# Masks added to bias tables by transfers, keys split once for two heads and stacked by transfers, in a two-layer decoder kernel

## The chip, the cores and the metric

The kernel runs on one core of a Trainium2 chip. PE (TensorE) multiplies, DVE (VectorE), ACT (ScalarE) and POOL (GpSimd) work element by element, and SP and POOL issue transfers (DMA) between DRAM and the on-chip memory. The metric is the time of one execution on the device in microseconds (us). The median of three runs before the change is 1831.09 us (1829.66 to 1831.96).

## The reference, cut to what matters

The input is one sequence of 512 positions with 1024 features, all in float32. Layer 0 has a feed-forward, the first ("hybrid") mixer and a second feed-forward; layer 1 has a feed-forward, the sliding mixer and a last feed-forward.

```python
h = h + 0.5 * swiglu(rmsnorm(h, g[0]), w1[0], w3[0], w2[0])
h = h + mixer(rmsnorm(h, g[1]))          # hybrid in layer 0, sliding in layer 1
h = h + 0.5 * swiglu(rmsnorm(h, g[2]), w1[1], w3[1], w2[1])
...
# the hybrid mixer: heads 0 to 7 (A) and 8 to 15 (B)
cq = rmsnorm(cq, cq_g); qb = cq @ wq_b; q_idx = cq @ wq_idx
o_a = dilated_mixture(qa, ka, va, table[:, :8])
sc = relu(einsum('bqhd,bsd->bqhs', q_idx, k_idx))         # 8 index heads
score = einsum('bqhs,bqh->bqs', sc, w_idx) * idx_scale    # one score per query and key
_, idx = top_k(score, 128)                                # 128 keys for each query
logits = q @ k[idx] * 64 ** -0.5 + bias                   # heads B see only these keys
o_b = softmax(logits) @ v[idx]
return concat(o_a, o_b) @ w_out
```

Every head has 64 features and a bias that depends on the distance of query and key. The B heads see only the selected keys, which the kernel does with masks of 512 x 512 instead of a gather.

## The kernel before

**Precision.** Operands of a product are split into a high and a low part (in `d4` and `s2` buffers of 32-bit numbers), and three products (low x high, high x low, high x high) replace one. In the listings these are L389, L390 and L391 for projections, L613 to L615 for the feed-forwards and L869 to L871 for the output projection. A weight of a mixer is loaded by SP (L338), cast to its high part on ACT (L356), copied with a factor of -1 (L357), and POOL then issues a transfer that adds the weight a second time to that negative (L359): what remains is the low part. A function `unit` with `lands=True` does this.

**Order.** Everything is emitted as operations of a planner (`Plan`). It takes them by due time `v`, keeps for each engine a modelled clock, and gives out buffers from pools: 58 slots of `s2` (128 x 512), 20 of `d4` (128 x 1024), 8 banks, and 2 value buffers `v` in a pool of their own. `LIMIT` says how many of a kind may be held, `RESERVE` how many slots a kind must leave free. The order that comes out is fixed, and each engine runs its instructions in that order. So an instruction that waits holds up all behind it on its engine, and so does a transfer on SP's or POOL's queue. A load is given the slot of a buffer that another instruction still reads and waits for that.

**Entry of a mixer.** The last feed-forward products of w2 give the eight chunks of x one after another. For each, DVE adds (L685), ACT scales it (L410) and squares it (L426), DVE makes the low part (L411) and adds up the squares (L427). L452 is a product with ones that sums the squares over the features. It needs the last chunk's L427. From it DVE computes the root (L435 to L441), PE and ACT spread it (L457, L462), and the projections are multiplied by it.

**First mixer.** `hybrid` (L879) does the index scores (L964 on PE, L967 on ACT, L971 to L978 on DVE), and then eight rounds of two heads: `project(j)` makes values, keys and queries, `attend(j)` two heads, `out_proj` a share of the output. In the queue of DVE between these stands the selection: for each of three blocks of 128 queries (256, 384 and 512 keys; the first block needs none) 16 times MAX8 (L986) and MATCH_REPLACE8 (L988). `close` makes a bf16 mask (L994) from what was replaced. Tables of the bias are loaded by `toeplitz` (L691, one transfer of 256 KB a head).

In `head`, each block of queries has two products of keys and queries (L780, L781), then L787 on DVE adds the bias table and takes the minimum. For the eight B heads (j of 4 and more) a third product, of the identity `identb` with the mask (L783), adds the mask to the scores on PE, for 256, 384 and 512 keys. ACT takes the exponential, DVE the reciprocal (L806), ACT or POOL scale (L817, L813), PE transposes (L829), L845 and L846 multiply with the values.

**Keys.** `k_stack` (L713) makes of one projection two stacks, one for each head, each with the keys (high and low) in both halves of the partitions, because queries hold their high part in one half and their low part in the other. Per pair: one product (L717), two casts of 64 x 512 (L399, ACT), two copies into the other half (L725 on ACT or L728 on POOL), four subtractions of 64 x 512 (L325, DVE or POOL). It is called eight times here and once in `sliding` (L1044).

## Time and profile before

| | |
|---|---|
| median of the runs | 1831.09 us (1829.66 to 1831.96) |
| the profiled execution | 1832.38 us, its span 1830.6 us |
| granted TensorE clock, mean | 0.995 |
| busy: PE, DVE, ACT, POOL | 1807.2, 1319.3, 969.2, 170.5 us |
| share of the chain that ended last: PE, DVE, ACT, DMA | 89%, 4%, 3%, 2% |

The profile is of one execution. "Idle before" is the time an engine stood still before an instruction, with what ended it. Busy times of PE are of pipelined products whose ends are modelled: one product of 512 columns is shown as 0.39 us long, and in a dense stretch they follow each other every 0.23 us.

### The profile page before, as it was taken

What the parts mean: (1) busy time and instruction counts of PE and PEld (TensorE: products, weight loads), DVE (VectorE), ACT (ScalarE), POOL (GpSimd) and SP (SyncE); (2) the same over time, 40 slices, a digit from 0 to 9 for tenths busy, and PEclk for the clock granted to TensorE, in tenths of its full rate; (3) what the DMA queues carried; (4) which work ended last, traced back from release to release, by engine and by line L of the source; (5) the groups of instructions that cost most, each with busy time, mean ns of one, the idle gap of its engine ahead of it and who ended that gap; (6) DMA issues with size and microseconds to landing.
All of it is one profiled execution on the core that took longest, in us unless ns stands there. A gap on an engine that the chain in (4) does not pass through costs nothing.

```text
span 1830.6 us, 28269 instructions
## 1 busy us (share of the span) xinstructions
PE 1807.2 (99%) x11036; PEld 1612.7 (88%) x11036; DVE 1319.3 (72%) x2225; ACT 969.2 (53%) x1600; POOL 170.5 (9%) x228
## 2 busy tenths in 40 slices
PE   9999999999999999999999999999999999999997
PEld 6889989888878889998998989989788889899896
DVE  8575857559977897586588866848468798577483
ACT  6343625658768555253355534625679755255263
POOL 2100000115524000000000000000124200000000
PEclk9999999999999999999999999999999999999999
DMA  6713423785745314232343224313844523243231
GB/s 215 245 58 114 122 64 113 198 209 119 162 112 138 103 48 126 92 105 81 109 117 97 83 91 127 118 56 105 229 95 102 150 70 116 70 127 116 70 104 46
DMA packets 75141, 211.55 MB, mean 116 GB/s; under 512 B 12976, under 2 KB 17168, under 8 KB 75008
## 3 DMA queue, kind: packets, MB, share of 16 engines
q1 hardware_dynamic: 58176, 176.88, 30.6%
q0 software_dynamic: 16688, 32.85, 9.8%
q8 instruction: 86, 1.41, 0.3%
q14 instruction: 47, 0.39, 0.1%
q10 hardware_dynamic: 144, 0.03, 0.0%
HBM read 205.92 MB, written 8.47 MB: 117 GB/s over the span
## 4 chain that ended last, share of the span: by engine, by line
PE 89%; DVE 4%; ACT 3%; DMA 2%; issue 1%; POOL 0%; SPq 0%; DVEq 0%; ACTq 0%; POOLq 0%
PE ps L389 14%; PE ps L390 14%; PE ps L391 14%; PE ps L613 12%; PE ps L615 12%; PE ps L614 12%; DVE d L325 1%; PE ps L869 1%; PE ps L870 1%; PE ps L871 1%; PE ps L829 1%; ACT s L796 1%; DMA d<-in_w 1%; PE ps L1155 1%; PE ps L1157 1%
## 5 line engine op out<-in xcount | busy, mean ns | idle before, releaser
L325 DVE TENSOR_TENSOR d<-d,d 128x1024 fp32r<-128x1024 f32 (+3 forms) x415 | 448.8, 1096 | 186.6 <-ACT d L346 138.3
L346 ACT CAST d<-d 128x1024 fp32r<-128x1024 f32 (+3 forms) x415 | 388.0, 949 | 328.6 <-DMA d<-in_w 209.0
L613 PE MATMUL ps<-s,d 128*128 128x256 f32 x1904 | 539.5, 283 | 0.0
L615 PE MATMUL ps<-s,d 128*128 128x256 f32 x1904 | 538.8, 283 | 0.0
L614 PE MATMUL ps<-s,d 128*128 128x256 f32 x1904 | 538.8, 283 | 0.0
L389 PE MATMUL ps<-s,d 128*128 128x512 f32 (+1 forms) x1252 | 496.0, 396 | 2.2 <-DVE d L325 2.0
L390 PE MATMUL ps<-s,d 128*128 128x512 f32 (+1 forms) x1252 | 489.8, 391 | 0.4 <-DVE s L411 0.3
L391 PE MATMUL ps<-s,d 128*128 128x512 f32 (+1 forms) x1252 | 489.2, 391 | 0.0
L613 PEld LDWEIGHTS ps<-s,d 128*128 128x128 f32 x1904 | 365.4, 192 | 0.5
L614 PEld LDWEIGHTS ps<-s,d 128*128 128x128 f32 x1904 | 365.4, 192 | 0.4
L615 PEld LDWEIGHTS ps<-s,d 128*128 128x128 f32 x1904 | 365.4, 192 | 0.0
L391 PEld LDWEIGHTS ps<-s,d 128*128 128x128 f32 (+1 forms) x1252 | 235.8, 188 | 50.2
L389 PEld LDWEIGHTS ps<-s,d 128*128 128x128 f32 (+1 forms) x1252 | 236.2, 189 | 49.7 <-DVE d L325 2.9
L390 PEld LDWEIGHTS ps<-s,d 128*128 128x128 f32 (+1 forms) x1252 | 236.2, 189 | 46.9 <-DVE s L411 1.2
L626 ACT COPY d<-ps 128x512 f32<-128x512 f32 x136 | 79.8, 587 | 250.0 <-PE ps L615 249.7
L685 DVE SCALAR_TENSOR_TENSOR s<-ps,s 128x512 f32<-128x512 f32 x88 | 60.7, 690 | 140.9 <-PE ps L391 140.9
L325 DVE TENSOR_TENSOR s<-s,s 128x512 fp32r<-128x512 f32 (+2 forms) x190 | 126.4, 675 | 8.8 <-ACT s L399 6.4
L565 DVE TENSOR_TENSOR d<-d 128x512 f32<-128x512 f32 x136 | 91.6, 688 | 2.3
L565 DVE TENSOR_TENSOR d<-d,d 128x512 f32<-128x512 f32 x136 | 90.2, 687 | 1.5
L629 DVE TENSOR_TENSOR d<-ps,d 128x512 f32<-128x512 f32 x102 | 70.1, 687 | 16.8 <-PE ps L615 16.1
L359 POOL DMA_DIRECT2D d<-in_swa_in x10 | 8.7, 865 | 731.6 <-DMA d<-in_swa_in 693.2
L356 ACT CAST d<-d 128x1024 fp32r<-128x1024 f32 (+3 forms) x69 | 55.0, 807 | 32.6 <-DMA d<-in_swa_in 13.4
(152 smaller groups left out, 1929.9 us busy)
## 6 DMA issues: line engine op xcount, KB each, us to landing
d<-in_w SPq DMA_DIRECT2D x238, 512.0 KB, 3.7
d<-in_w SPq DMA_DIRECT2D x32, 384.0 KB, 3.1
d<-in_hyb_in SPq DMA_DIRECT2D x22, 512.0 KB, 5.5
d<-in_hyb_in POOLq DMA_DIRECT2D x22, 512.0 KB, 6.7
d<-in_swa_in SPq DMA_DIRECT2D x10, 512.0 KB, 5.5
d<-in_swa_in POOLq DMA_DIRECT2D x10, 512.0 KB, 7.6
tab<-rv POOLq DMA_DIRECT2D x4, 1024.0 KB, 20.0
s<-tab SPq DMA_DIRECT2D x16, 256.0 KB, 5.5
```

The source lines that it names most:

```text
L325: return lambda: eng.tensor_sub(out(), a(), b().bitcast(F32))
L346: alts = [("act", ns[0](n), lambda: nc.scalar.copy(hl.at(0, o), raw.t[:, c]))]
L389: nc.tensor.matmul(o, wl, xh.t, start=i == 0, stop=False)
L390: nc.tensor.matmul(o, wh, xl.t, start=False, stop=False)
L391: nc.tensor.matmul(o, wh, xh.t, start=False, stop=i == n - 1)
L565: return lambda: eng.tensor_add(o.t[:, oc], a.t[:, ac], o.t[:, oc])
L613: nc.tensor.matmul(o, wl, xh, start=start and m == 0 and k == 0, stop=False, skip_group_check=True)
L614: nc.tensor.matmul(o, wh, xl, start=False, stop=False, skip_group_check=True)
L615: nc.tensor.matmul(o, wh, xh, start=False, stop=k == 3, skip_group_check=True)
L626: self.act(act_ns(S, False), lambda: nc.scalar.copy(view(q, c), bank(ps)), [ps], [(q, key)])
L629: self.dve(vec_ns(S), lambda: nc.vector.tensor_add(view(q, c), bank(ps), view(q, c)), [ps, (q, key)], [(q, key)])
L685: self.dve(dve_ns(S), lambda ps=ps, x=x: nc.vector.scalar_tensor_tensor(x.t, ps.t, 0.5, x.t, op0=OP.mult, op1=OP.add), [ps, x], [x])
```

## The change

1. The masks leave PE. `close` now writes the mask in float32 over the score buffer. For the B heads `masked` takes the place of `toeplitz`: SP loads the table's part for each of the four blocks (128, 256, 384, 512 columns), and for the three larger POOL issues a transfer inside the chip that adds the mask to the table. `head` reads one such table for each block, and L783 and `identb` go.
2. `k_stack` makes the product, one cast of 128 x 512 and one subtraction of 128 x 512 into a buffer `kt`; four transfers of 256 KB, issued by SP, lay the two stacks out of it. The subtraction has no alternative on POOL any more. `q_stack` is still split between DVE and POOL, now by the planner in all rounds.
3. Value buffers come from the `d4` pool, which has 22 slots.
4. Loads with `lands=True` are due 1000 earlier and are planned with a latency of 4000 instead of 2100.

The core of the diff:

```diff
-CAPACITY = {"s2": SLOTS, "ps": 8, "d4": 20, "v": 2}
+CAPACITY = {"s2": SLOTS, "ps": 8, "d4": 22}
+LIMIT: 'toepb': 3, 'toepc': 3, 'kt': 2, 'v': 2
...
-            self.lo_lands(hl, self.load(src, v - 7000, n), src, n, v)
+            self.lo_lands(hl, self.load(src, v - 8000, n, lat=LAT), src, n, v)
...
+    def masked(self, tab, h, masks):
+        b, c = Buf("d4", "toepb", (128, 1024)), self.s2("toepc")
+        out = [(c, 384), (c, 0), (b, 512), (b, 0)]
+        for qb, (buf, at) in enumerate(out):
+            n = (qb + 1) * 128
+            key = (buf, at)
+            self.dma(lambda buf=buf, at=at, n=n: nc.sync.dma_start(buf.t[:, at:at + n], tab[h][:, S - n:]),
+                     [("tab", S, h // 4)], [key], n * 512, self.vt - MASKED)
+            if masks[qb] is not None:
+                self.dma(lambda buf=buf, at=at, n=n, m=masks[qb]: nc.gpsimd.dma_start(
+                    buf.t[:, at:at + n], m.t[:, :n], accum_op=OP.add), [masks[qb], key], [key], n * 512,
+                    self.vt - MASKED + 2000, "pool")
...
-    def k_stack(self, ps, rows, pool=True):
+    def k_stack(self, ps, rows):
+        f, both = self.s2("tmp"), Buf("d4", "kt", (128, 1024), F32R)
+        self.dve(vec_ns(S), lambda: nc.vector.tensor_mul(f.t, ps.t, rows.t), [ps, rows], [f])
+        hi, lo = Half(both, 0), Half(both, 1)
+        self.hi(hi, f)
+        self.sub(lambda: lo.t, lambda: f.t, lambda: hi.t, [f, hi], [lo], S, ns=vec_ns)
         k = []
         for h in range(2):
-            kh, kl = self.pair("k")
-            self.hi(kh, f, own, (kh, 0))
...
+            b = Buf("d4", "k", (128, 1024), F32R)
+            kh, kl = Half(b, 0), Half(b, 1)
+            for i in range(2):
+                self.dma(lambda b=b, i=i, h=h: nc.sync.dma_start(
+                    b.t[i * 64:i * 64 + 64].bitcast(F32), both.t[h * 64:h * 64 + 64].bitcast(F32)),
+                    [hi, lo], [(kh, i), (kl, i)], 262144)
...
-        v = Buf("v", shape=(128, 8, 2, 64), dtype=F32R)
+        v = Buf("d4", "v", (128, 8, 2, 64), F32R)
...
-                if m is not None:
-                    nc.tensor.matmul(ps.t[:, :n], self.identb, m.t[:, :n], start=False, stop=True)
...
-                masks[qb] = Buf("s2", "mask", (128, S), BF16)
+                masks[qb] = sc
...
+MASKED = 10000.0
+LAT = 4000.0
```

In the changed kernel's listings L699 and L702 are the loads and the mask transfers of `masked`, L742 the key transfers, L798 what L787 was, L824 what L813 was, L793 and L794 what L780 and L781 were.

**The sliding mixer's loads on SP.** The rows of SP before L452 of the sliding mixer; a buffer's number counts up in the order in which the planner hands buffers out, `tab1` rows are tables. Before:

```order
L338 DMA d4_13001<-in_swa_in 128x1024
L693 DMA s2_13021<-tab1_70 128x256
L338 DMA d4_13037<-in_swa_in 128x1024
L338 DMA d4_13071<-in_swa_in 128x1024
L338 DMA d4_13116<-in_swa_in 128x1024
L338 DMA d4_13173<-in_swa_in 128x1024
```

And now:

```order
L338 DMA d4_12992<-in_swa_in 128x1024
L338 DMA d4_13026<-in_swa_in 128x1024
L709 DMA s2_13042<-tab1_70 128x256
L338 DMA d4_13062<-in_swa_in 128x1024
L338 DMA d4_13096<-in_swa_in 128x1024
L338 DMA d4_13142<-in_swa_in 128x1024
```

`d4_13071` and `d4_13062` are both the eighth load of that mixer, and in both kernels its cast is the last on ACT ahead of the last chunk's L410. The first was handed out after the last w2 product's bank (`ps_13043`), and its transfer waits for the 39th product before L452; the second was handed out ahead of that bank (now `ps_13064`) and waits for the 59th.

**The first mixer's entry on ACT.** `s2_174` and `s2_173` are the last chunk of x in the two kernels. Before:

```order
L356 CAST d4_3413<-d4_3403 128x1024
L410 ACTIVATE s2_3420<-s2_152,gcol_71 128x512
L426 ACTIVATE s2_3425<-s2_152 128x512
L357 ACTIVATE d4_3443<-d4_3403 128x1024
L410 ACTIVATE s2_3454<-s2_174,gcol_71 128x512
L426 ACTIVATE s2_3459<-s2_174 128x512
L356 CAST d4_3490<-d4_3486 128x1024
L357 ACTIVATE d4_3492<-d4_3486 128x1024
```

And now:

```order
L410 ACTIVATE s2_3427<-s2_151,gcol_71 128x512
L426 ACTIVATE s2_3432<-s2_151 128x512
L356 CAST d4_3439<-d4_3416 128x1024
L357 ACTIVATE d4_3445<-d4_3416 128x1024
L356 CAST d4_3460<-d4_3452 128x1024
L357 ACTIVATE d4_3467<-d4_3452 128x1024
L410 ACTIVATE s2_3472<-s2_173,gcol_71 128x512
L426 ACTIVATE s2_3478<-s2_173 128x512
```

The last chunk's two rows stood ahead of the cast of the next load; two loads' casts now stand between the last chunk but one and the last, and the second of these loads (`d4_3452`) waits for the 44th product before L452.

**The end of the selection on DVE.** In the changed kernel, from the last step of the selection on (`s2_3972` is the last block's score and then its mask, `d4_601` the table of head 8 for the last block):

```order
L999 MATCH_REPLACE s2_3972<-m8_5275,s2_3972 128x512
L1005 TENSOR_SCALAR s2_3972<-s2_3972 128x512
L325 TENSOR_TENSOR d4_5287<-ps_5277,d4_5287 128x8x64
L733 TENSOR_TENSOR s2_5306<-ps_5250,s2_3554 128x512
L717 SCALAR_TENSOR_TENSOR s2_5323<-ps_5302,s2_3703 128x512
L325 TENSOR_TENSOR d4_5317<-s2_5306,d4_5317 128x512
L325 TENSOR_TENSOR s2_5330<-s2_5323,s2_5330 64x512
L325 TENSOR_TENSOR s2_5335<-s2_5323,s2_5335 64x512
L798 ISA s2_5352,stat_5186<-ps_5198,d4_601 128x512
```

Between the mask and the add of head 8's table stands the transfer of the mask into `d4_601`; before, the mask went from L994 straight into L783 on PE.

## Rows read from the trace of the kernel before

**Rows 1.** The page's first part: busy us (share of the span) and instructions.

```profile
PE 1807.2 (99%) x11036; PEld 1612.7 (88%) x11036; DVE 1319.3 (72%) x2225; ACT 969.2 (53%) x1600; POOL 170.5 (9%) x228
```

**Rows 2.** Windows: stretch, its length, busy us of each engine, granted clock, DMA.

```profile
391.50:522.65 131.15, 127.85 (x651) 106.47 (x650) 122.81 (x324) 100.43 (x209) 60.66 (x68) 1.00 0.61 142
522.65:600.00 77.35, 74.56 (x403) 60.30 (x402) 57.66 (x132) 60.64 (x140) 29.91 (x41) 1.00 0.55 126
...
1326.20:1332.50 6.30, 6.30 (x19) 5.33 (x20) 1.97 (x12) 2.00 (x2) 0.86 (x1) 0.50 0.84 166
1332.50:1340.00 7.50, 7.50 (x39) 6.21 (x38) 3.46 (x5) 5.09 (x8) 1.72 (x2) 1.00 0.49 119
```

**Rows 3.** Timeline of PE at a mask: start, length, engine, line, operation.

```profile
525.32 0.40 PE L781 MATMUL ps<-d,s 128*128 128x512 f32 x1
525.56 0.39 PE L783 MATMUL ps<-s,identb 128*128 128x512 bf16 x1
```

**Rows 4.** Groups by form, 385 to 600: count, busy us, mean ns of one.

```profile
L325 POOL TENSOR_TENSOR d<-s,d 64x512 fp32r<-64x512 f32 x17 | 23.8, 1402 | 3.2 <-ACT d L399 2.3
...
L325 DVE TENSOR_TENSOR d<-s,d 64x512 fp32r<-64x512 f32 x15 | 15.4, 1027 | 2.0 <-ACT d L399 1.8
L359 POOL DMA_DIRECT2D d<-in_hyb_out x16 | 13.9, 935 | 15.3 <-DVE s L851 7.0 <-ACT d L357 6.6 <-PE ps L781 1.5
...
L325 DVE TENSOR_TENSOR s<-s,s 128x512 fp32r<-128x512 f32 x7 | 5.2, 737 | 0.0
```

**Rows 5.** Transfers issued from 391.5 to 600: count, size, median us to landing.

```profile
d<-in_hyb_in SPq DMA_DIRECT2D x12, 512.0 KB, 5.2
...
d<-in_hyb_out SPq DMA_DIRECT2D x16, 256.0 KB, 3.2
d<-in_hyb_out POOLq DMA_DIRECT2D x16, 256.0 KB, 6.3
...
s<-s SPq DMA_DIRECT2D x12, 64.0 KB, 2.0
```

**Rows 6.** The same, issued from 520 to 524.

```profile
d<-in_hyb_out POOLq DMA_DIRECT2D x1, 256.0 KB, 8.9
```

**Rows 7.** Timeline of DVE at the selection's end.

```profile
522.21 0.43 DVE L994 TENSOR_SCALAR s<-s 128x512 bf16<-128x512 f32 x1
```

**Rows 8.** Timeline of PE behind it, with idle time and releaser.

```profile
530.80 0.88 PE L829 MATMUL ps<-ident,s 128*128 128x128 f32 x6 [1.42 <-ACT s L817]
```

**Rows 9.** Timelines of SP, ACT, DVE and PE at the sliding mixer's entry.

```profile
1313.78 0.33 SPq L338 DMA_DIRECT2D d<-in_swa_in  x1
1322.11 1.05 ACT L356 CAST d<-d 128x1024 fp32r<-128x1024 f32 x1 [4.31 <-DMA d<-in_swa_in]
1325.42 0.69 DVE L427 TENSOR_TENSOR s<-s,s 128x512 f32<-128x512 f32 x1
1326.16 1.87 PE L452 MATMUL ps<-ones,s 128*128 128x1 f32 x8 [3.57 <-DVE s L427]
```

**Rows 10.** The transfer issued at 1313.78: size, us to landing.

```profile
d<-in_swa_in SPq DMA_DIRECT2D x1, 512.0 KB, 8.2
```

**Rows 11.** Timelines of SP, ACT and PE at the first mixer's entry.

```profile
352.12 1.33 SPq L693 DMA_DIRECT2D s<-tab  x3
364.03 0.62 ACT L426 ACTIVATE s<-s 128x512 f32<-128x512 f32 x1
367.14 0.95 PE L452 MATMUL ps<-ones,s 128*128 128x1 f32 x8
370.24 1.05 ACT L356 CAST d<-d 128x1024 fp32r<-128x1024 f32 x1 [5.59 <-DMA d<-in_hyb_in]
```

**Rows 12.** The load issued on SP at 358.4: size, us to landing.

```profile
d<-in_hyb_in SPq DMA_DIRECT2D x1, 512.0 KB, 11.7
```

**Rows 13.** Timeline of PE in the sliding mixer: end of L457, first score product.

```profile
1334.21 0.60 PE L457 MATMUL ps<-ident,tiny 128*128 128x128 f32 x4
1346.73 0.22 PE L780 MATMUL ps<-d,s 128*128 128x128 f32 x1
```

More of the change, by code (lines that the diff above doesn't have):

```diff
@@ L331, in sub, with load @@
         return self.p.op(alts, r, w, self.vt if v is None else v)
-    def load(self, src, v, n=1024, pieces=1, halves=False, step=None):
+    def load(self, src, v, n=1024, pieces=1, halves=False, step=None, lat=2100.0):
         raw, m = Buf("d4", "wraw", (128, 1024)), n // pieces
@@ L338, in load @@
             self.dma(lambda c=c: self.nc.sync.dma_start(raw.t[:, c], src[:, c]), (), [(raw, 0), (raw, 1)] if halves else [(raw, i)], m * 512,
-                     v + i * (step or 3 * pe_ns(S) * m / 128))
+                     v + i * (step or 3 * pe_ns(S) * m / 128), lat=lat)
         return raw
@@ L711, in q_stack @@
         return q
-    def k_stack(self, ps, rows, pool=True):
+    def k_stack(self, ps, rows):
         nc = self.nc
-        f = self.s2("tmp")
-        self.dve(dve_ns(S), lambda: nc.vector.tensor_mul(f.t, ps.t, rows.t), [ps, rows], [f])
+        f, both = self.s2("tmp"), Buf("d4", "kt", (128, 1024), F32R)
[3 more added lines that the diff above has]
+        self.sub(lambda: lo.t, lambda: f.t, lambda: hi.t, [f, hi], [lo], S, ns=vec_ns)
         k = []
         for h in range(2):
-            own, oth = slice(h * 64, h * 64 + 64), slice(64 - h * 64, 128 - h * 64)
-            kh, kl = self.pair("k")
-            self.hi(kh, f, own, (kh, 0))
-            def dup_act(kh=kh, own=own, oth=oth):
-                nc.scalar.copy(kh.t[oth], f.t[own])
-            def dup_pool(kh=kh, own=own, oth=oth):
-                nc.gpsimd.tensor_scalar(kh.t[oth], f.t[own], 1.0, 1.0, op0=OP.mult, op1=OP.mult)
-            self.p.op([("act", act_ns(S), dup_act), ("pool", pool_ns(S), dup_pool)], [f], [(kh, 1)], self.vt)
-            for i, out in enumerate((own, oth)):
-                self.sub(lambda kl=kl, out=out: kl.t[out], lambda own=own: f.t[own],
-                         lambda kh=kh, own=own: kh.t[own], [f, (kh, 0)], [(kl, i)], S, pool)
+            b = Buf("d4", "k", (128, 1024), F32R)
[4 more added lines that the diff above has]
+                    [hi, lo], [(kh, i), (kl, i)], 262144)
             k.append((kh, kl))
@@ L757, in v_split, with head @@
         return v
-    def head(self, q, k, tt, v, vi, o, half, masks=None, band=None):
+    def head(self, q, k, tt, v, vi, o, half, band=None):
         nc = self.nc
@@ L946, in project @@
             V[j] = self.v_split(self.v_turned(ps, R))
-            K[j] = self.k_stack(proj(4 + j if j < 4 else 10 + j, pool=pool), R, pool or True)
+            K[j] = self.k_stack(proj(4 + j if j < 4 else 10 + j, pool=pool), R)
             if j < 4:
-                Q[j] = self.q_stack(proj(j, pool=pool), R, pool or True)
+                Q[j] = self.q_stack(proj(j, pool=pool), R)
             else:
-                Q[j] = self.q_stack(proj(0, cq, t["wq_b"][j - 4], 256, pool=pool), Rc, pool or True)
+                Q[j] = self.q_stack(proj(0, cq, t["wq_b"][j - 4], 256, pool=pool), Rc)
         masks = [None] * 4
@@ L1014, in attend @@
             for i in range(2):
-                self.head(Q[j][i], K[j][i], T.pop(0), V[j], i, o[j], i, masks if j >= 4 else None)
+                self.head(Q[j][i], K[j][i], T.pop(0), V[j], i, o[j], i)
                 if T_next:
-                    T.append(self.toeplitz(self.tab0, T_next.pop(0), S))
+                    h = T_next.pop(0)
+                    T.append(self.toeplitz(self.tab0, h, S) if h < 8 else self.masked(self.tab0, h, masks))
         o = []
@@ L1100, in tables @@
         self.dma(lambda: pool.dma_start(self.tri, t["tri"]), after, ["tri"], 65536, v, "pool")
-        self.act(250, lambda: nc.scalar.copy(self.identb, self.ident), ["ident"], ["identb"], v)
         self.dma(lambda: pool.dma_start(self.sinkp, bass.AP(
```

30 lines of the change are left out of this document (17 added, 13 removed).

## The prediction

> **What bounds the kernel now.** I read the page's busy times first. PE works in 1807.2 of 1830.6 us [rows 1], so the time is PE's own work plus 23.4 us of waits, and every other engine matters only where PE waits for it. A change can gain in three ways: less work on PE, fewer waits, or a clock that stays up. So I looked next at where PE waits. The windows show it for the first mixer [rows 2]: from its index scores to the end of the selection (391.5 to 522.65) PE misses 131.15 - 127.85 = 3.3 us, and from there to 600 another 77.35 - 74.56 = 2.8 us. In the first of the two DVE is busy for 122.81 of 131.15 us: the selection (top-k on DVE) sets when the masks of the last block are known, at 522.21 + 0.43 = 522.64 [rows 7].
>
> The largest single wait is elsewhere, at the entry of the sliding mixer, and I take it apart because the change touches the loads there. PE begins L452 only at 1326.16, after an idle 3.57 us, so it was free at 1322.6 [rows 9]. Backwards: L452 waits for L427 on DVE, that for the two ACT passes over the last chunk of x (L410, L426), and these stand on ACT behind the cast of a weight load, which began at 1322.11 after waiting 4.31 us for its transfer. That load was issued at 1313.78 [rows 9] and needed 8.2 us [rows 10]. Right behind the wait the granted clock is 0.50 from 1326.2 to 1332.5 and 1.00 again after it [rows 2], that is 1.2 instead of 2.4 GHz. Those 6.3 us of PE work would take 3.15 at full clock, so the entry costs 3.57 + 3.15 = 6.7 us.
>
> **Masks off PE.** Each of the eight masked heads loses three bf16 products. By the ends of two neighbours, 525.32 + 0.40 = 525.72 and 525.56 + 0.39 = 525.95 [rows 3], the one with 512 columns occupies PE for 0.23 us; by columns the three (256, 384, 512) cost 0.23 x 1152 / 512 = 0.52, and eight heads 4.1 us. PE is dense there, so nothing hides them: **-4.1**. The 24 weight loads of the identity go beside other work and count nothing.
>
> **The masks' new way.** A table is loaded in four pieces, and three pieces get the mask added by a transfer that GpSimd issues. For the last block the chain is: selection closes, GpSimd issues (0.9 [rows 4]), the transfer lands, DVE adds the table to the scores, and that frees a bank of scores that PE wants. Before, PE needed only the close. A 256 KB transfer of this queue lands in 6.3 us as a median in this mixer [rows 5], and in 8.9 when several are queued, as at 520 to 524 [rows 6]. The DVE work up to the close changes little: six subtractions of 64x512 at 1.03 go (-6.2), five of 128x512 at 0.74 come (+3.7), and six low parts of queries that GpSimd made come, at 1.03 at most (+6.2) [rows 4]. That is at most +3.7, and I put the close at 524.5 instead of 522.6. With the issue and the landing the mask is in the table at 531.7 to 534.3, and the bank is free 0.7 later. By the order PE does 15 us of projections between the first five score banks of heads 8 and 9 and the next ones, and I expect it there at 531.5 to 532. So it waits 0.4 to 3.5, and I take 1.5. DVE itself waits at that add, and behind it stand the other adds of heads 8 and 9 and a product for the values of pair 5; PE needs the probabilities of head 8 some 5 us later, so their way (exponential, reciprocal, scaling) is covered or late by as much as the bank is. GpSimd's queue also holds normalisations of probabilities behind these transfers; a transfer there waits for the load of its table, and later heads may wait up to 2 us in two places for that. I take nothing for it and keep 4 for the range.
>
> **Waits of the first mixer.** Before the close PE waited 3.3 us. DVE and GpSimd, behind which it stands there, lose work or get it earlier: the GpSimd subtractions of 1.40 us are gone [rows 4], and per pair ACT casts one 128x512 instead of two pieces and copies nothing. I take 1.5 of the 3.3 as left. Of the 2.8 behind it, half is one wait for a normalisation at 530.80 [rows 8], which the projections before it now cover, so 1.5 stay, with the 1.5 of the masks' chain on top. That is 4.5 instead of 6.1: **-1.6**, between -4.5 and +4.
>
> **Keys by transfers.** A pair's keys are now split once at 128x512 and laid into two stacks by four transfers of 256 KB on SP, nine times. This lengthens the way from the subtraction to the first product with the keys. By the order and the durations above, what PE does in between is worth 16, 15, 14, 9, 8.2, 8.5, 13 and 17 us for the eight pairs. In the sliding mixer the whole way from L457's end (1334.8) to the first score product (1346.73) is 11.9 us [rows 13], of which copy, product, cast and subtraction take some 3.6, so 8.3 are left. No row shows a copy of this shape. The nearest: 64 KB inside the chip 2.0, 256 KB from DRAM 3.2 on SP's queue [rows 5]. The lower bound for four is 3.2 plus three issues of 0.44 (three tables are issued in 1.33 [rows 11]), thus 4.5; the upper is four at 3.2 one behind another, 12.8. I take 6.5, nearer to the lower end, since the four are under way together like those tables: hidden everywhere, with **+0.5** for a place where other transfers run beside them.
>
> The Trainium skill speaks against this (SBUF — State Buffer, section "Door 1: The DMA port swizzle"): a transfer that reaches 64 partitions only uses half the ports and runs at some 196 GB/s, and its section "Can I just issue two DMAs to hit both halves?" says that two such transfers serialize. An estimate by that page is 1.3 us each and about 7.3 for four with its fixed 2 us, against my 6.5: still under 8.2, but with other transfers beside them no longer. No run here shows it yet.
>
> **Sliding entry.** The value buffers move to the shared pool of big buffers (20 to 22), and the loads are planned earlier. The eighth load of that mixer, whose cast stands ahead of the last chunk's L410 in both kernels, waits for a buffer that PE frees. By the counts that its wait names, this was 39 products before L452. The trace has 1322.6 - 1313.8 = 8.8 us for them, 0.226 each [rows 9]. It is now 59 products before, 13.3 us. The way from landing to L452 took 1326.16 - (1313.78 + 8.2) = 4.2. With 8.2 for the transfer 12.4 are needed and 13.3 are there. So the wait goes, and with it the fall of the clock: **-6.7**. Next late would be the last chunk itself, but where ACT doesn't wait, as in the first mixer, L426 ends at 364.65, 2.5 us before L452 [rows 11].
>
> **First mixer's entry.** Here the order turns the other way. Before, the last L410 and L426 ended at 364.65, ahead of a cast that waited until 370.24 for a load, and PE reached L452 at 367.14 without a wait [rows 11]. Now two casts of loads stand ahead of that L410, and the second load is freed 44 products (9.9 us) before L452, because three big and three small buffers are held by tables of heads 8 to 10 loaded in the first feed-forward. 9.9 - 4.2 = 5.7 us are left for its transfer. Rows near it: 5.2 as the median inside the mixer [rows 5], 8.2 for the sliding mixer's late one [rows 10], and 11.7 for a load issued at 358.4 behind three tables [rows 11, 12]. Now one table is ahead of it, so I take 7.3, between the first two: **+1.6** of wait, from 0 to 6, and no fall of the clock, which the trace shows only behind the wait of 3.57.
>
> **Sum.** The profiled execution took 1832.4 (span 1830.6). 1832.4 - 4.1 - 1.6 + 0.5 - 6.7 + 1.6 = 1822.1. The median of the runs is 1.3 lower than that execution, so **1821**. With the terms' own ends the case reaches from 1816 to 1825.
>
> **Rivals.** (a) The first mixer's entry takes over the stall: the load needs 11.7, as at 358.4, PE waits 6.0, and the clock falls for another 3.15 as at 1326. That is 7.5 more than the 1.6 taken, 1828 to 1829; with 10 us it is 1827. For it: by the order four tables and five loads are asked for within a few products of each other there, and the pattern on ACT is that of the sliding entry. Against it: fewer tables ahead. (b) Slower than before: the key copies land late. Their place is the four tight covers 9, 8.2, 8.5 and 8.3; if four copies take L, PE waits 4 L - 34 in all. At L = 10 that is 6 us, 1827; at L = 12 it is 14, 1835, and from there on the kernel is slower; at 12.8 it is 17, 1838. For it: 8.9 for one transfer in a queue [rows 6]. Against it: 3.2 for 256 KB on SP's queue [rows 5]. The rule of the Trainium skill quoted above, from the page SBUF — State Buffer, would work in this direction. (c) The change doesn't do what it says on PE: the products of the masks go, but the chain close, transfer, DVE holds PE in their place, and the mixer's waits stay at 6.1 plus 4. Then the 5.7 of the first two terms are lost: 1827, from the sliding entry alone.
>
> **Chances.** The forecast 0.56; (a) 0.16; (b) 0.16, half of it at or above 1835; (c) 0.12. A measurement of this kernel can tell some 0.2%, 3.7 us, from no change, so faster means below 1827.4 and slower above 1834.8. Faster gets the forecast and about half of the others, which lie around that line: 0.74. The rest of (a), (b) and (c) below 1834.8 is 0.17, slower 0.09. The range 1816 to 1829 holds the forecast with its ends and most of (a), (c) and the mild half of (b).
>
> **What would show it.** Masks: PE's work in the mixer smaller by 4. Sliding entry: no wait at L452 and a granted clock of 1.00 throughout; if the wait is there, that step is wrong. First entry: a wait of 0 to 6 at L452 near 367, and whether the clock falls behind it. Keys: waits of the first score products for transfers. Masks' chain: waits of score or transpose products between 525 and 560. The prediction fails most likely by waits for transfers at several of these places at once.

## The result, and the profile after

The changed kernel takes 1844.9 us (median of 4 runs, 1841.8 to 1847.7) against 1831.5 before: a ratio of 1.0071 with the interval 1.0053 to 1.0089. It is slower by 0.7%, where 1821 was forecast, and it lies outside the range. The profiled execution took 1847.7, with a span of 1845.8; before, the span was 1830.6.

The first look is at where the 15.2 us between the two spans arise. I cut each span at the same five places of the program: the transposes that open the first mixer's index scores (L932 before, L943 after; about 1 us ahead of the first score product), the end of that mixer's output projection, the first score product of the sliding mixer, the end of its output projection, the end. The windows of the kernel before (stretch, length, busy us of PE, PEld, DVE, ACT, POOL with counts, granted clock, DMA share, GB/s):

```profile
0.00:389.80 389.80, 386.12 (x2251) 338.74 (x2252) 259.23 (x386) 187.53 (x263) 26.18 (x38) 1.00 0.49 146
389.80:624.30 234.50, 228.09 (x1174) 188.12 (x1173) 201.49 (x488) 175.01 (x372) 90.58 (x109) 1.00 0.56 132
624.30:1346.70 722.40, 718.71 (x4595) 656.37 (x4594) 507.92 (x713) 341.89 (x468) 9.94 (x11) 1.00 0.36 107
1346.70:1469.10 122.40, 122.25 (x712) 105.89 (x711) 104.27 (x276) 105.33 (x275) 41.96 (x68) 1.00 0.47 113
1469.10:1830.60 361.50, 352.04 (x2310) 323.60 (x2309) 246.37 (x364) 159.44 (x225) 1.81 (x2) 0.99 0.28 90
```

The same of the kernel after:

```profile
0.00:401.40 401.40, 390.84 (x2248) 340.34 (x2249) 258.70 (x386) 185.29 (x260) 25.32 (x37) 0.98 0.48 144
401.40:642.20 240.80, 228.49 (x1153) 191.21 (x1152) 195.56 (x485) 173.05 (x368) 71.05 (x92) 0.98 0.83 193
642.20:1360.10 717.90, 715.77 (x4595) 653.56 (x4594) 508.57 (x713) 339.60 (x468) 9.48 (x11) 1.00 0.37 109
1360.10:1482.50 122.40, 122.24 (x711) 106.05 (x712) 105.74 (x278) 105.48 (x274) 41.11 (x67) 1.00 0.48 116
1482.50:1845.80 363.30, 351.97 (x2310) 323.45 (x2309) 245.72 (x362) 157.35 (x224) 1.81 (x2) 0.99 0.27 88
```

By stage that is +11.6, +6.3, -4.5, 0.0 and +1.8. The third stage holds the sliding entry, and there the mechanism that was forecast is seen: no wait at L452 as in [rows 9], and a granted clock of 1.00 where [rows 2] had 0.50. The stage as a whole gains 4.5 of the 6.7, with a new wait of 0.9 for key copies at its end (1360.06). The second stage, in which the masks, the keys and the queues were to bring some 5 us together, has lost 6. The first stage has lost most: it is the first feed-forward, on which the prediction says nothing, with the first mixer's entry at its end. In the second stage the DMA share has gone from 0.56 to 0.83.

Second, the waits of PE in the span after (engine, line, for whom: us in total, times, longest):

```profile
PE ps L389 <- ACT s L399: 5.5, 1, 5.5
PE ps L793 <- DMA d<-d: 4.8, 1, 4.8
PE ps L840 <- POOL s L824: 3.9, 1, 3.9
```

Their places, in timelines of PE (start, length, operation, idle before it and releaser):

```profile
113.07 0.79 PE L389 MATMUL ps<-s,d 128*128 128x512 f32 x1 [5.50 <-ACT s L399]
...
554.05 0.44 PE L793 MATMUL ps<-d,s 128*128 128x128 f32 x1 [4.75 <-DMA d<-d]
...
594.13 1.29 PE L840 MATMUL ps<-ident,s 128*128 128x128 f32 x5 [3.88 <-POOL s L824]
```

Around each of the three the granted clock is 0.50, that is 1.2 instead of 2.4 GHz: for 10.2 us from 109.5, for 6.8 from 553.3, for 3.4 from 594.2. But in the first two the clock is down already while PE still stands, and lost is only half of what PE worked in them (windows as above):

```profile
109.50:119.70 10.20, 6.21 (x14) 4.59 (x15) 10.20 (x21) 6.64 (x12) 0.00 (x0) 0.50 0.00 0
553.30:560.10 6.80, 6.05 (x22) 5.13 (x23) 2.73 (x9) 2.81 (x7) 5.21 (x7) 0.50 1.10 269
594.20:597.60 3.40, 3.40 (x12) 2.92 (x13) 2.01 (x4) 2.30 (x4) 3.40 (x6) 0.50 0.94 164
```

That half is 3.1, 3.0 and 1.7, so the three waits cost 8.6, 7.8 and 5.6. (The expectations below say 11, 8 and 6: there the whole stretches were counted as work.) I followed each back.

**At 113.** The cast at L399 came late because DVE and ACT had worked through weights that had landed late. ACT stood 16.6 us for the first of them:

```profile
82.72 2.09 ACT L346 CAST d<-d 128x1024 fp32r<-128x1024 f32 x2 [16.60 <-DMA d<-in_w]
```

SP's queue shows why:

```profile
43.98 2.01 SPq L338 DMA_DIRECT2D d<-in_w  x2
62.38 0.33 SPq L699 DMA_DIRECT2D s<-tab  x1
...
70.00 0.43 SPq L699 DMA_DIRECT2D d<-tab  x1
71.28 4.66 SPq L338 DMA_DIRECT2D d<-in_w  x4
```

Between 46.0 and 62.38 SP issues nothing. It stands before the first of twelve loads (L699) of the masked tables of heads 8 to 10, which the new code asks for in the first feed-forward, and waits for GpSimd to have written these tables to DRAM (`tab<-rv` are the transfers that write them; SP's waits: us in total, times, longest):

```profile
SPq L699 <- DMA tab<-rv: 16.3, 1, 16.3
```

The weights' loads behind them go out from 71.28 on and land 10.2 to 11.4 us later. Before, SP's queue in this stretch held weights alone, seven loads from 45.29 to 74.69, the second to fourth of them at 54.2, 54.7 and 58.0:

```profile
45.29 29.40 SPq L338 DMA_DIRECT2D d<-in_w  x7
```

**At 554.** The score products of head 10 wait for the key copies of pair 5 (L742), which SP issues between table loads:

```profile
541.66 1.94 SPq L742 DMA_DIRECT2D d<-d  x2
543.69 2.40 SPq L699 DMA_DIRECT2D d<-tab  x1
546.14 2.30 SPq L742 DMA_DIRECT2D d<-d  x1
...
549.18 1.16 SPq L699 DMA_DIRECT2D d<-tab  x2
550.38 0.52 SPq L742 DMA_DIRECT2D d<-d  x1
```

From the first copy's issue to the last one's landing (557.70) that is 16.0 us, where 6.5 was taken. PE did not wait for all four: it goes on at 554.05, as the third copy lands, which was issued at 546.14 (count, size, us to landing):

```profile
d<-d SPq DMA_DIRECT2D x1, 256.0 KB, 7.8
```

So the first head waits for the first and the third copy, here 12.3 us from the first issue. In all runs that issue the copies from SP, a wait for them at a pair's first score product ends within 0.3 us of the third copy's landing; the text goes on to give the time of all four, as the prediction does.

**At 594.** A normalisation of probabilities (L824) stands on GpSimd's queue behind a transfer that adds a mask (L702), and this waits 9.2 us for the load of its table:

```profile
592.59 0.86 POOL L702 DMA_DIRECT2D d<-s  x1 [9.20 <-DMA d<-tab]
593.17 0.90 POOL L824 TENSOR_SCALAR s<-s,stat 128x384 f32<-128x384 f32 x1
```

### The profile page after: what moved, and what is told of

It reads as the page before. It is cut to its first block, busy times and chain, and to the rows that moved or that the text cites. A ratio compares the mean times of both kernels' runs of the same rounds, so it can differ in the third digit from the quotient of the medians.

```text
span 1845.8 us, 28321 instructions
## 1 busy us (share of the span) xinstructions
PE 1809.3 (98%) x11012; PEld 1614.6 (87%) x11012; DVE 1314.3 (71%) x2222; ACT 960.8 (52%) x1591; POOL 148.8 (8%) x209
## 4 chain that ended last, share of the span: by engine, by line
PE 87%; DVE 7%; ACT 2%; DMA 2%; issue 1%; SPq 0%; POOL 0%; DVEq 0%; ACTq 0%; POOLq 0%
PE ps L390 14%; PE ps L389 14%; PE ps L391 14%; PE ps L613 12%; PE ps L615 12%; PE ps L614 12%; DVE d L325 1%; PE ps L840 1%; PE ps L880 1%; PE ps L881 1%; PE ps L882 1%; DVE s L999 1%; DVE m L997 1%; DVE s L325 1%; PE ps L1165 1%
## 5 line engine op out<-in xcount | busy, mean ns | idle before, releaser
L346 ACT CAST d<-d 128x1024 fp32r<-128x1024 f32 (+3 forms) x415 | 385.7, 948 | 402.2 <-DMA d<-in_w 187.9
L325 DVE TENSOR_TENSOR s<-s,s 128x512 fp32r<-128x512 f32 (+2 forms) x197 | 130.3, 676 | 8.3 <-ACT s L399 3.7
L807 ACT ACTIVATE s<-s,stat 128x256 f32<-128x256 f32 (+3 forms) x128 | 65.9, 516 | 11.5 <-DVE stat L798 11.3
```

Of the source, the lines that this page charges most:

```text
L325: return lambda: eng.tensor_sub(out(), a(), b().bitcast(F32))
L346: alts = [("act", ns[0](n), lambda: nc.scalar.copy(hl.at(0, o), raw.t[:, c]))]
L807: nc.scalar.activation(x, x, AF.Exp, bias=st.t[:, qb:qb + 1], scale=-1.0, accum_out=st.t[:, 4 + qb:5 + qb])
```

## The experiments

**Theory A**: these three queue waits make the loss. **Rivals**: B, the key copies over 64 partitions are slow wherever they are; C, the moved loads cost as much elsewhere; D, the masks' transfers cost as such. All runs, medians in us and ratio to the kernel before on the same chip:

| run | what it is | median | ratio (95%) |
|---|---|---|---|
| x1_ahead | change, masked tables asked for later | 1838.5 | 1.0041 (1.0028 to 1.0054) |
| x2_source | change, early tables from input data | 1837.1 | 1.0035 (1.0024 to 1.0047) |
| x5_loads | before, loads' part alone | 1823.3 | 0.9953 (0.9938 to 0.9968) |
| x6_masks_loads | x5 and masks | 1831.9 | 1.0004 (0.9993 to 1.0015) |
| k1_keys_loads | x5 and keys | 1836.1 | 1.0035 (1.0024 to 1.0046) |
| k2_keys_act | k1, copies issued by ACT | 1832.8 | 1.0011 (1.0000 to 1.0022) |
| k3_half | k1, copies of half the bytes | 1827.5 | 0.9982 (0.9970 to 0.9994) |
| k4_128 | k1, copies as 128x512 | 1830.1 | 0.9995 (0.9980 to 1.0009) |
| l1_lat | before, earlier loads alone | 1825.9 | 0.9969 (0.9958 to 0.9980) |
| d1_drain | x5, 24 small transfers more | 1826.8 | 0.9977 (0.9967 to 0.9986) |
| g1_norm_act | x6, normalisations on ACT | 1828.4 | 0.9994 (0.9984 to 1.0005) |
| g2_late_plan | x6, tables planned with 9 us | 1828.6 | 0.9992 (0.9982 to 1.0002) |
| g3_both | x6, both | 1831.6 | 1.0006 (0.9996 to 1.0015) |
| z1_mended | change, three mends | 1852.8 | 1.0124 (1.0107 to 1.0141) |
| z2_mended_128 | z1, copies as 128x512 | 1835.0 | 1.0032 (1.0022 to 1.0042) |
| a1_copies_128 | change, copies as 128x512 | 1835.4 | 1.0020 (1.0009 to 1.0030) |
| a2_128_source | a1 and x2 | 1828.7 | 0.9986 (0.9976 to 0.9996) |
| a3_masks_aside | change, masks written aside | 1834.4 | 1.0015 (1.0005 to 1.0024) |

Executions of kernels with such waits scatter by up to 13 us (x1_ahead 1831.1 to 1843.8, with a mean granted clock between 0.992 and 0.996; its profiled one is the lowest), the four of x5_loads by 1.4. So prices are taken from medians, and the profiles tell what waits for what. Between runs that did not share a chip the ratios give somewhat other prices: 15.0 us for the keys' part (12.8 below), 7.3 for the copies' shape in k4_128 (6.0), 9.7 for k3_half (8.7), 6.6 for x2_source (7.8). Several medians lie outside every range that was expected of them: x1_ahead, g1_norm_act and g2_late_plan between their two ranges, g3_both above both, a2_128_source and a3_masks_aside below theirs, z2_mended_128 between its two; a1_copies_128, d1_drain, k4_128 and x2_source miss the nearest range by less than 1 us.

### The early tables on SP's queue

x1_ahead gives the masked tables the bound that the other tables have:

```diff
-AHEAD = {'toep': 30000.0, 'sx': 8000.0}
+AHEAD = {'toep': 30000.0, 'toepb': 30000.0, 'toepc': 30000.0, 'sx': 8000.0}
```

> The changed kernel, with the early tables of the masked heads held back by the same bound of 30000 that the other tables have, so that none is asked for in the first feed-forward. Theory A (the loss is made of three waits in queues: SP's queue blocked by early tables in the first feed-forward, 11 us; key copies of pair 5, 8 us; a normalisation behind table transfers on GpSimd's queue, 6 us): no wait near 113 us and no fall of the clock there, 1832 to 1836 us. Theory B (the 64-partition key copies and the transfers as a whole cost, spread over the kernel; the wait near 113 us is made by something else, such as casts placed late by the planner): 1841 to 1848 us, the wait stays.

x2_source leaves every instruction in its place and takes the wait away:

```diff
+        src = self.t["hyb_in"][h - 8] if h < 11 else tab[h]
-  ... nc.sync.dma_start(buf.t[:, at:at + n], tab[h][:, S - n:]),
+  ... nc.sync.dma_start(buf.t[:, at:at + n], src[:, S - n:S]),
```

> The changed kernel with every instruction in the same place; only the early tables of heads 8 to 10 are read from input data that is in memory from the start, and not from the tables that the kernel makes first (left out: the true bias of heads 8 to 10). Theory A: SP no longer stands before these loads, the loads of the first feed-forward go out 10 us earlier, the wait near 113 us goes with its fall of the clock: 1832 to 1837 us. Rival: the wait comes from the buffers which the early tables hold, or from the order of the casts on ACT and DVE; both are the same here, so the time stays at 1842 to 1848 us.

The first feed-forward is back to 389.2 and 390.5 us, and the wait near 113 is gone in both. Nothing but the source differs in x2_source, so neither the buffers that the tables hold nor the order of the casts made the wait: it is SP standing before loads of data that don't exist yet. Price 7.8 us (6.4 by x1_ahead), where the profile's wait and fall make 8.6; both medians lie above what I expected (x2_source by 0.1).

### Each part alone

x5_loads has the earlier plan of the loads and the shared pool, and nothing else of the change; l1_lat has the first alone:

```diff
-            self.lo_lands(hl, self.load(src, v - 7000, n), src, n, v)
+            self.lo_lands(hl, self.load(src, v - 8000, n, lat=4000.0), src, n, v)
-CAPACITY = {"s2": SLOTS, "ps": 8, "d4": 20, "v": 2}
+CAPACITY = {"s2": SLOTS, "ps": 8, "d4": 22}        (x5_loads only)
```

> The kernel before with only the earlier plan of the loads at a mixer's entry and the values in the pool of big buffers; masks and keys as before. Theory A: the sliding mixer's entry has no wait of 3.6 us and no fall of the clock, worth 6.7 us, and nothing else changes: 1823 to 1828 us. Rival C (moving the loads costs as much elsewhere, by other transfers or by the first mixer's entry): 1829 to 1834 us.

> The kernel before with only the earlier plan of the loads at a mixer's entry; the values keep their own two buffers. By the order, 60 products stand between the freeing of the late load's buffer and the first projection of the sliding mixer, as in x5_loads, against 40 before. If that count decides: the wait of 3.6 us and the clock fall at the sliding entry are gone, 1822 to 1827 us. If the shared pool is needed for it: 1829 to 1833 us, with the wait in its place.

x5_loads is faster than both kernels, by 0.5% than the one before; theory C falls. The sliding entry has no wait and no fall in either run; the stage from the first mixer's end to the sliding scores takes 716.1 us in x5_loads and 715.2 in l1_lat, 6 to 7 less than before. So the earlier plan alone gives that gain, and the pool perhaps 2.5 to 3 more, inside the first mixer (230.8 us against 235.2 in these profiles); the intervals of the two ratios overlap, so the pool's share is not shown.

x6_masks_loads adds the masks' part to x5_loads (with the bound of x1_ahead), k1_keys_loads the keys' part:

> The changed kernel with the keys made as before, and with the bound of 30000 on the masked heads' tables: thus masks by transfers and the loads' part alone. Theory A: 6.7 us of the sliding entry and 4.1 us of the masks are gained, the wait behind GpSimd's queue (up to 6 us) can remain: 1820 to 1828 us, faster than both kernels. Rival (the chain of masks by transfers holds PE in the place of the products): 1829 to 1835 us.

> Keys by transfers and the loads' part, with the masks as products on PE as before. The loads' part alone gave 1823.3. Theory A (the copies are late only where tables and other transfers of SP's queue stand before them, above all with the masked heads' tables): 1822 to 1827 us, waits of the score products for the key copies under 4 us in all. Theory B (the copies over 64 partitions are slow by themselves and late at most pairs): 1830 us or more, with waits of 2 us or more at the first score products of at least three pairs.

Both parts cost: the masks 8.6 us, the keys 12.8. For the masks the rows explain it. PE's waits in x6_masks_loads:

```profile
PE ps L844 <- POOL s L828: 7.1, 4, 3.5
```

These 7.1, two falls of the clock in the mixer (3.4 lost) and 1.9 at the end of the program (below), less the 4.1 forecast for the products, make 8.3. Only one of the falls (539.5) stands behind a wait for GpSimd, the one of 2.5; the other (515.6) follows three waits for DVE of 0.3 to 0.9, and the longest wait, 3.5 us at 582, has none. For the keys, PE's waits in k1_keys_loads:

```profile
PE ps L776 <- DMA d<-d: 7.9, 4, 4.1
```

A fall of 3.4 us behind the longest (1.7 lost) makes 9.6 of 12.8; another fall follows two waits of 0.8 and 1.1 for DVE at 518 to 520. No table with masks stands on SP there, so theory A has no cause for it, and B is nearer: the copies are late at four places without the tables, and the time is the one that B expected, though only one of the four waits is over 2 us.

### The key copies: queue, bytes or shape

k2_keys_act issues the copies from ACT; k3_half carries half the bytes, k4_128 the same bytes over all partitions, both with every instruction in its place:

```diff
-  nc.sync.dma_start(b.t[i*64:i*64+64], both.t[h*64:h*64+64])
+  nc.scalar.dma_start(... the same ...)                               (k2_keys_act)
+  nc.sync.dma_start(b.t[i*64:i*64+64, :512], both.t[h*64:h*64+64, :512])  (k3_half)
+  nc.sync.dma_start(b.t[:, i*512:i*512+512], both.t[:, i*512:i*512+512])  (k4_128)
```

> As k1_keys_loads, but the four key copies of a pair are issued by ACT, where they stand behind no table or weight load of SP's queue; sizes and number are the same. Theory A (the place on SP's queue makes them late): waits for key copies under 1 us each, 1820 to 1825 us, and not above k1_keys_loads. Theory B (the transfer itself): the same waits as in k1_keys_loads, the same time within 3 us; and a rival to both is that ACT, which stands while it waits for the subtraction, holds its own casts up: then over 1828 us.

> As k1_keys_loads (1836.1 us; from the first copy's issue to the last one's landing 7.2 to 13.4 us, mean 10.1, waits for copies 7.9 us), every instruction in its place, but each key copy carries half the bytes, 64x512 and not 64x1024 (left out: the low parts of the keys, for which the high parts are read twice). If the time of a copy goes by its bytes: the four land in 5 to 7 us, no wait for copies over 1 us, 1823 to 1829 us. If it goes by the count of transfers and by what else is under way on the chip's transfer engines: the four still take 8 us or more, 1832 to 1837 us.

> As k1_keys_loads, every instruction in its place, the same four copies of 256 KB, but as 128x512 and not 64x1024, so that each reads and writes all partitions (left out: the stacking; both heads get the same rows). The Trainium skill (SBUF — State Buffer, section "Door 1: The DMA port swizzle") says that a transfer that reaches 64 partitions only uses half the ports: by it four copies would now land in some 5 to 7 us, waits for copies under 2 us in all, 1824 to 1830 us. Rival: the shape matters little, the bytes and the neighbours do: 8 us or more for the four, 1833 to 1838 us.

The place that tells most is pair 5, where at most the end of one load is under way as the copies go out. Copies issued there (count, size, median us to landing), in k1_keys_loads:

```profile
d<-d SPq DMA_DIRECT2D x4, 256.0 KB, 4.7
```

in k4_128:

```profile
d<-d SPq DMA_DIRECT2D x4, 256.0 KB, 2.4
```

and in k3_half:

```profile
d<-d SPq DMA_DIRECT2D x4, 128.0 KB, 2.3
```

From first issue to last landing the four take 7.9, 4.2 and 4.2 us there. As 64x1024 they land at 544.59, 545.86, 548.10 and 549.37, 1.3 to 2.2 us apart; as 128x512 0.6 to 0.7 apart, as they were issued. So the same bytes take twice as long over 64 partitions, one copy behind the other. Over all nine places the mean is 10.1 us (k1), 8.2 (k4) and 7.6 (k3), in k4_128 above the 5 to 7 expected: beside other transfers all become slower. The shape is worth 6 us here, half the bytes 8.7. The place on the queue is worth 3.4: k2_keys_act waits 2.5 us for copies instead of 7.9, though its four take no less (10.8 in the mean); DVE then holds PE for 3.1 at 615.69, with a fall of 6.8 us, behind a cast on ACT that waits 2.8 for a weight load. Theory B is right for this part; A's claim that only queues made the copies late falls.

### The masks' queue, and the end of the program

The edits of g1_norm_act and g2_late_plan on x6_masks_loads; g3_both has both:

```diff
-  self.p.op([("pool", ..., np_), ("act", ..., na)], ...)
+  self.p.op(([] if isinstance(tt, list) else [("pool", ..., np_)]) + [("act", ..., na)], ...)   (g1)
-  [key], n * 512, self.vt - MASKED)
+  [key], n * 512, self.vt - MASKED, lat=9000.0)      (g2, with MASKED 17000 and the
                                                       adding transfers at their old due time)
```

> Masks by transfers and the loads' part (1831.9 us when last run), now with the normalisation of the masked heads' probabilities on ACT alone, so that none stands behind a table transfer on GpSimd's queue. Theory A (that queue is what the masks' part costs): the waits of 3.5 us at 582 and 2.5 us at 538 for a normalisation on GpSimd go, with the falls of the clock behind them: 1822 to 1827 us. Theory D (the transfers themselves, or the chain from the closed selection over the transfer to DVE, cost PE as much): 1829 to 1834 us, with new waits for DVE or for transfers in the same place.

> Masks by transfers and the loads' part (1831.9 us), the normalisations where the planner wants them, but the planner is told that a table's load takes 9 us to land and not 2.1, and asks for it 7 us earlier; the adding transfers keep their due time. Theory A (the wait on GpSimd's queue comes from an order planned with transfers that land four times sooner than they do): the normalisations stand ahead of the adding transfers that wait, 1821 to 1827 us. Theory D: 1829 to 1834 us.

> Masks by transfers and the loads' part, with both mends: normalisations of the masked heads on ACT, and the tables' loads planned with 9 us. Each alone gave 1828.5 (1831.9 without). If they mend different waits: 1823 to 1826 us, near the loads alone (1823.3), since the 4.1 us of the masks' products off PE stand against 1.9 at GpSimd's last drain. If they mend the same wait: 1827 to 1830 us.

Either mend takes the waits for GpSimd's normalisations away. By the medians it gives 3.3 us, by the ratios some 2 with intervals that overlap, and so less than the 5 to 10 expected and hardly clear of noise; new waits appear, for DVE at the mixer's end (2.0 and 2.8 us at 610) and, in g2_late_plan, at L860 (2.3). Both together give nothing: PE then waits 4.5 us at L860, the products with the values, for the low parts of the transposed probabilities on DVE, and the clock falls twice. The trace shows why DVE is later: it stands before the add of a table (L802) until a mask's transfer has landed. In g3_both, DVE's waits of this kind, and the one ahead of the longest wait at L860 (598.84):

```profile
DVE s L802 <- DMA d<-s: 8.0, 3, 3.6
597.48 0.69 DVE L802 CUSTOM_DVE_ANT_0 s<-ps,d 128x512 f32<-128x512 f32 x1 [3.58 <-DMA d<-s]
```

In g2_late_plan it is 7.6, in x6_masks_loads 0.7, in x5_loads none. So with the queue mended the wait for the mask moves from GpSimd to DVE.

The last stage is 1.4 to 2.8 us longer in every kernel with masks on GpSimd's queue. Its program ends with a drain; the instructions of the last line, before (count: min/median/max ns):

```profile
L1359 POOLq DRAIN  x3: 46/93/4598, 1825.2 to 1830.3; - x3
```

and after:

```profile
L1373 POOLq DRAIN  x3: 46/97/6557, 1838.5 to 1845.6; - x3
```

d1_drain adds 24 transfers of 1 KB in the third feed-forward to x5_loads, where PE waits for none of them:

```diff
+  for k in range(24):
+      self.dma(lambda k=k: self.nc.gpsimd.dma_start(self.extra[:, 2*k:2*k+2], self.t["cqg"]), [self.x[0]], ...)
```

> As x5_loads (1823.3 us), with 24 more transfers of 1 KB on GpSimd's queue in the third feed-forward, where nothing waits for them. In the traces GpSimd's last drain takes 4.60 us with 92 transfers on its queue and 6.56 with 116, in every kernel; with 116 the program ends 1.9 us later behind its last output. If the number of transfers makes this: drain 6.5 to 6.6 us, 1825 to 1826 us. If it is the kind (transfers that add) or the bytes: drain 4.6, 1823 to 1824 us.

```profile
L1366 POOLq DRAIN  x3: 46/98/6189, 1817.7 to 1824.3; - x3
```

The drain grows by 1.6 us and the last stage by 2.1 (361.4 to 363.5); the median grows by 3.5, of which the profile shows 1.0 between the mixers. So more transfers on that queue lengthen the end, nearly as much without bytes or addition as with them.

### Each cause taken out of the change itself

z1_mended puts the bound of x1_ahead and both mends of the masks' queue into the whole change, z2_mended_128 has the copies as 128x512 on top:

> The whole change with the three mends of its queues: bound of 30000 on the masked heads' tables, their loads planned with 9 us, their normalisations on ACT; the key copies as they are. x1_ahead, with the first mend alone, gave 1838.5. If GpSimd's queue is the second cause: 1830 to 1836 us, with waits for the key copies as the main rest. If the key copies take all: 1836 us or more.

> As z1_mended, every instruction in its place, with the key copies as 128x512 and not 64x1024 (left out: the stacking). If the copies' shape is the third cause: 5 to 7 us under z1_mended, as between k1_keys_loads and k4_128, 1824 to 1830 us. If what is left comes from elsewhere: within 3 us of z1_mended.

Mending made it worse, by 14 us against x1_ahead: four waits of 2.2 to 5.7 us at the first score products, 16.0 in all, each ending as a third key copy lands; the four copies of a pair take up to 15.6. In that order GpSimd issues five adding transfers from 556.67 to 558.82, just as SP issues copies from 557.63 on. z2_mended_128, in the same order, gives back 17.8. So the order alone does not decide what the copies cost; their shape does too. Since the mends move other work, I then took each cause out with every instruction of the changed kernel in its place: a1 and a2 by the lines of k4_128 and x2_source, a3 by

```diff
-  nc.gpsimd.dma_start(buf.t[:, at:at + n], m.t[:, :n], accum_op=OP.add)
+  nc.gpsimd.dma_start(self.aside[(h - 8) * 3 + qb - 1][:, :n], m.t[:, :n])
```

> The changed kernel (1844.9 us), every instruction in its place, the key copies as 128x512 and not 64x1024 (left out: the stacking). If the copies' shape costs here what it cost between k1_keys_loads and k4_128: 1836 to 1840 us, and the wait of 4.8 us near 554 for a copy under 2. If the copies are late by SP's queue and not by their shape: 1842 to 1846 us.

> As a1_copies_128, and the early tables of heads 8 to 10 read from input data as in x2_source (left out: the stacking and the true bias of those heads). If the two causes add: 1837.1 less 5 to 7, 1830 to 1833 us. If not: 1835 us or more.

> The changed kernel (1844.9 us), every instruction in its place, but GpSimd's transfers of the masks write to a place of their own in DRAM instead of adding to the tables, so that they wait for no table and no addition waits for them (left out: the masks). If GpSimd's queue is a cause of its own: the wait of 3.9 us near 594 and its clock fall go, 1838 to 1841 us. If another wait takes its place, such as a key copy of the same pair: 1843 to 1846 us.

From 1844.9, the copies' shape is worth 9.5 us, the early tables 7.8, both together 16.2 (they add), and the masks' waits and additions 10.5. The three sum to 27.8, but they overlap: in a1 the wait at 554 is 2.3 and GpSimd's wait at 594 is 2.0 without a fall behind it, though nothing was edited there, and in a3 the waits for copies are 1.3 at most. That slow copies hold the tables up, and tables the copies, is read from SP's queue at 541 to 551 and was not tested by itself. In a3 GpSimd still issues 24 transfers of the same sizes, and the DMA share of the mixer is 0.80: what waited for the masks' transfers cost the time, and not that they run, which speaks against rival D but for the drain (these transfers go to DRAM, though). The three together were not run.

## Why the prediction was wrong

**Sliding entry, -6.7: right**, by its mechanism and nearly by its size: -7.6 for the loads' part, of which 6 in the stage of that entry. **First mixer's entry, +1.6 (0 to 6): right in size**: in the changed kernel no wait at L452 and 1.0 just before it for the same chunk, 0.4 to 1.5 at L452 in its parts. There the clock does sometimes fall, as at 370.0 in g1_norm_act behind a wait of 1.4, which I had excluded.

**Masks off PE, -4.1: the products are gone, the size not seen in full.** PE's work in the first mixer is 226.6 us in x5_loads and 227.9 less 3.4 of lost clock, 224.5, in x6_masks_loads: -2.1. Each stop adds some busy time, so the rest can't be told apart. Against it stand 1.9 us for GpSimd's drain, which I did not know of.

**First mixer's waits, -1.6 (-4.5 to +4): failed, by a term set to nothing.** The step "a transfer there waits for the load of its table ... I take nothing for it and keep 4 for the range" had the mechanism and set it to zero. It is 5.6 us at 594 alone; in x6_masks_loads it is 7.1 of waits and one fall. The masks' chain itself, taken at 1.5, holds DVE's add for 2.3 us (L798) and PE not at all in the changed kernel, so rival (c) is not seen there; its mechanism shows in g2_late_plan and g3_both. I had priced the loads by [rows 5], the medians of a mixer with a DMA share of 0.56. The same kind of transfer in the kernel after (512 KB of weights by SP, 256 KB by GpSimd):

```profile
d<-in_hyb_in SPq DMA_DIRECT2D x13, 512.0 KB, 7.2
...
d<-in_hyb_out POOLq DMA_DIRECT2D x16, 256.0 KB, 8.1
```

against 5.2 and 6.3 in [rows 5]. Beside the change's own transfers most others of this stage took longer (the 64 KB copies stay at 2.0), so the prices read before the change were too low.

**Keys by transfers, +0.5: the term that was mis-sized.** "I take 6.5, nearer to the lower end, since the four are under way together": they are not, they land one behind the other. The four take 10.0 us in the mean in the kernel after (6.8 to 16.0). The formula of rival (b), 4L - 34, gives 6 for L = 10; k1_keys_loads waits 7.9 in four places, and the clock fall behind the longest, which the rival had not priced, brings it to 9.6. In the changed kernel the late place is pair 5, one of the four tight covers I had named, with L = 16.0; the formula has 7.5 for it and PE waits 4.8, since it needs only the third copy, after 12.3. In k1_keys_loads, in its own order, the late places are pairs 0, 1, 6 and 7. The covers, too, were read too long: for pairs 0, 6 and 7 I had 16, 13 and 17 us, and from the first copy's issue to the point where PE begins to wait the traces show 10.7 (pair 0, the changed kernel), 6.8 and 7.7 (pairs 6 and 7 of a3_masks_aside, in the same order). So there were more tight places than four. The rule of the Trainium skill that I quoted (SBUF — State Buffer, "Door 1: The DMA port swizzle") agrees with the trace: 4.7 us against 2.4 for the same bytes. My estimate of 7.3 for four by that page is near what the least disturbed fours take, 6.8 to 7.9. I wrote that with other transfers beside them the cover would no longer do, and then did not act on it.

**Not in the prediction: the first feed-forward**, 7.8 us. I had seen that "three big and three small buffers are held by tables of heads 8 to 10 loaded in the first feed-forward" and counted only the buffers. The order showed twelve loads on SP's queue ahead of the weights, and that they read a table which GpSimd has yet to write; the question who stands behind them was not asked. With its 7.8 the forecast would have been 1829, near no change.

Of the rivals (b) came closest: its mechanism is there, at L = 10 instead of 12. Not one late place decided, but three of about equal price: as a rough check, 1821 + 9.5 + 7.8 + 10.5 = 1849, less overlaps, against 1845 measured.

## What to carry to other kernels

For every transfer that a change adds, read three things off the order: what data it waits for, what stands behind it on its queue, and how many bytes its stretch moves already. A queue that waits for data delays all loads behind it, also in a stage that the change doesn't name, and prices read from a quiet stretch don't hold in a loaded one. When a change bundles several parts, run each alone: here one part gains 0.5%, one loses as much and one 0.7 to 0.8%.

## What the runs showed of the hardware

- A copy inside the chip of 256 KB takes 4.7 us as 64x1024 and 2.4 as 128x512 where little else is under way, and 64x1024 copies land 1.3 to 2.2 us apart.
- With the DMA share of the mixer at 0.83 instead of 0.56, a 512 KB load by SP takes 7.2 us as a median instead of 5.2, and a single issue on SP's queue took up to 2.4 us (at 543.69) instead of 0.3 to 0.5.
- GpSimd's drain at the end takes 4.60 us with 92 transfers on its queue in the whole program, and 6.1 to 6.6 with 116. With 92 it ends 0.2 us behind the landing of the last output (1829.8 and 1829.5 before), with 116 in the changed kernel 2.2 behind it (1845.1 and 1842.8).
- The granted clock fell to 0.50 around waits of 5.5, 4.8 and 3.9 us, for 10.2, 6.8 and 3.4 us, and in g1_norm_act behind one of 1.4 (368.6), while the one of 1.42 in [rows 8] and one of 3.5 (x6_masks_loads, 582.4) had none. At 109.5 it fell 3.6 us before PE began again. With half of PE's work in the stretch counted as lost, the three waits cost 1.4 to 1.6 times their length.
